# Two chained transformer blocks on one core: affine rows held back, roots as a power on GpSimd, and a new split of transposed rows

## The chip, the core and the metric

The kernel runs on one core of a Trainium2 chip. The metric is the time of the device for one execution, in microseconds (us). The engines are named as in the profile: PE is the matrix engine (TensorE), DVE the vector engine, ACT the scalar engine, POOL is GpSimd, SP issues transfers. Each engine works through its own list of instructions in order; semaphores tie the lists together.

## What is computed

Two blocks are chained over 512 image tokens and 256 context tokens of width 1024, all in float32. Cut to what matters here:

```
# first block, two layers
for i in (0, 1):
    y = mixer_i(modulate(h, m[0], m[1]))             # retention; neighbourhood attention
    h = layer_norm(alpha * h + m[2] * y, ln_g[i, 0], ln_b[i, 0])
    f = swiglu(modulate(h, m[3], m[4]), w13[i], w2[i])   # (silu(a @ gate) * (a @ up)) @ w2
    h = layer_norm(alpha * h + m[5] * f, ln_g[i, 1], ln_b[i, 1])
# second block, one layer
z = rms_norm(x, g_mix) @ w_in                        # windowed and block attention, a linear recurrence
x = x + merged(z) @ w_out
u = rms_norm(x, g_ffn) @ w_gu
x = x + (silu(gate) * up) @ w_down                   # then a last rms_norm

def layer_norm(x, g, b):
    xc = x - mean(x);  return xc * rsqrt(mean(xc * xc) + 1e-5) * g + b
def rms_norm(x, g):
    return x * rsqrt(mean(x * x) + 1e-6) * g
```

The image and the context tokens have their own modulation m; in the second layer of the first block the context's rows are needed only as keys and values.

## The kernel before

**Products.** A float32 product is made of three faster ones. Each operand is split into a high part that the fast format holds exactly and a low part, the rest; `mm3` and `t_mm` add high x high, high x low and low x high in a bank. A weight slab comes as one transfer (`raw`, 128x1024) and is split in two halves: ACT copies the high part, DVE subtracts it (`w<-raw,w`), in some stretches POOL. Eight banks hold results. Tokens stand in six tiles of 128 (0 and 1 context, 2 to 5 image), four where only image tokens are left.

**Order.** `body` does not issue instructions but records them into a `Recorder`. Its `plan` is a list scheduler: an instruction becomes ready when its predecessors have ended by a table of costs (`cost`) and handovers (`LAG`), and each engine takes the earliest in program order among the ready ones; `issue` writes them out in order of the planned starts. So each engine's order is decided by these costs, and all instructions have one line in the profile, that of the replay. `after(n, f)` puts a piece of program n ticks of the clock later (a tick comes after a piece of a product).

**Transitions.** The residual rows are R[i][half], token tile by token tile, and the next products need them normalised and transposed. `bound` runs a row product in two half sweeps. The last slabs of the second run tile by tile, and after each tile a chain of small work follows: `add_gated` (DVE multiplies the bank by the gate, `gt<-bank,gbc`; POOL adds it, `R<-gt,R`), statistics (`bn`, `mv`), `rsqrt`, and the normalised rows (`R<-R,mv,rstd`). `rsqrt` is written for DVE: a first guess from the bits, then three Newton steps, in all eight instructions on 128x1 (`rs_g`, `rs_h`, `rs_t`, `rstd`) behind one that adds eps. In pairs the tiles go to `to_T`: PE transposes (`bank<-ident,R`), ACT scales and shifts (`tt`), DVE casts the high part (`act<-tt`), POOL subtracts the low part (`act<-tt,act`). `t_gemm_first` then multiplies the first slabs by the context part, then by the image part in two halves of 256 columns, so that it can begin before the last pair is there; `r_sweep(first=...)` does the same token tile by token tile.

R itself is kept with the affine of the layer norm, which the next residual needs: `affine_rows` multiplies and adds on POOL (`R<-R,bc`), 128x512 four times a tile. `affine_later` puts it behind the transition by `after`, from the third tick.

The transitions are named here T1 (retention's output product to feed-forward, at 700 us), T2 (feed-forward to neighbourhood attention, 1262), T3 (attention's output to feed-forward, 1640), T4 (first block to second, 2015; here two norms follow each other, a layer norm and an RMS norm, whose rows are `X`, `chain_h`), and T5 (second block's mixer to its feed-forward, 2560).

Of the kernel before, what the change touches and what calls it, by code (L numbers as in the profile page):

```python
# [51 lines left out]
class Recorder:  # L52
# [34 lines left out]
    def add(self, eng, meth, fn, a, k):  # L87
# [5 lines left out]
        for w, aps in ((False, ins), (True, outs)):  # L93
            for ap in aps:
# [18 lines left out]
                keep.append((i, w, r))  # L113
                self.hist[n] = keep
        self.ops.append((eng, meth, fn, a, k, preds, list(dict.fromkeys(names)), i + self.bias))

    LAG = {("vector", "tensor"): 260, ("scalar", "tensor"): 281, ("gpsimd", "tensor"): 203,
# [4 lines left out]
    def cost(self, op):  # L122
# [13 lines left out]
        if eng == "tensor":  # L136
            if meth == "transpose":
                return n / 1.2, 0
            return (max(n * 4 / 2.4, 213) if a[2].dtype == F32 else n / 2.4) + 2.5, 0
        ptr = sum(isinstance(v, bass.AP) for v in k.values())  # L140
# [8 lines left out]
        fast = meth in ("tensor_scalar", "tensor_copy", "memset") and not ps  # L149
        return n / (1.92 if fast else 0.96) + 69 + 60 * ptr, 0  # L150

    def plan(self):
# [40 lines left out]
        win, busy, warm, carry_end = 0, 0.0, False, 0.0  # L193
        start, stop, tfin = [0.0] * N, [0.0] * N, {}

        def push(t, kind, x):
# [15 lines left out]
        while nd < N:  # L212
# [12 lines left out]
            while progressed:  # L225
                progressed = False
                for e in engs:
# [41 lines left out]
                    start[i] = now  # L269
                    end = now + hold  # L270
                    free[e] = end
                    if op[1] == "dma_start":
# [176 lines left out]
def body(nc, tc, io, sp, wp, pp, dp, order, stop=None, dbg=None):  # L449
# [66 lines left out]

    def rsqrt(out, v):
        g = small([128, 1], "rs_g", dt=I32)
        h = small([128, 1], "rs_h")
        t = small([128, 1], "rs_t")  # L520
        DVE.tensor_scalar(g, v.bitcast(I32), -0.5, float(0x5F3759DF), op0=ALU.mult, op1=ALU.add)
        DVE.tensor_scalar(h, v, -0.5, None, op0=ALU.mult)
        y = g.bitcast(F32)
        for it in range(3):
            DVE.scalar_tensor_tensor(t, y, y, h, op0=ALU.mult, op1=ALU.mult)
            DVE.scalar_tensor_tensor(out if it == 2 else y, t, 1.5, y, op0=ALU.add, op1=ALU.mult)

# [18 lines left out]
    ones = kp.tile([128, 128], F32, name="ones", tag="ones", bufs=1)  # L546
    DVE.memset(ones, 1.0)
    ones_r = kp.tile([128, 128], F32R, name="ones_r", tag="ones_r", bufs=1)
    ACT.activation(ones_r, ones, AF.Copy)
# [106 lines left out]
    def t_gemm_first(keys, act, segs):  # L656

        wts = [ws.get(*k) for k in keys]
        parts = []
        for s in segs:  # L660
            if s[0] not in parts:
                parts.append(s[0])
        banks = [out_banks(parts) for _ in keys]
        for part, c0, c1, pre in segs:
            if pre is not None:
                pre()
            for b, w in zip(banks, wts):
# [48 lines left out]

    def add_gated(R, i, half, b, gate):
        if gate is None:
            DVE.tensor_tensor(R[i][half], b, R[i][half], op=ALU.add)
        else:  # L720
            t = S(name="gt")
            DVE.tensor_tensor(t, b, gate[half], op=ALU.mult)
            POOL.tensor_tensor(R[i][half], t, R[i][half], op=ALU.add)

# [7 lines left out]
    def ln_rstd(i):  # L732
        mv = small([128, 2], "mv", bufs=8)
        DVE.bn_aggr(mv, stats[i])
        v = small([128, 1], "lnv", bufs=8)
        DVE.tensor_scalar(v, mv[:, 1:2], 1e-5, None, op0=ALU.add)
        rstd = small([128, 1], "rstd", bufs=8)
        rsqrt(rstd, v)
        return mv, rstd
# [6 lines left out]
    def rms_rows(R, i, n=1024):  # L746
        ss = small([128, 2], "ss", bufs=8)
        for half in range(2):
            j = S(name="sq")
            ACT.activation(j, R[i][half], AF.Square, accum_out=ss[:, half:half + 1])  # L750
        v = small([128, 1], "rv", bufs=8)
        DVE.tensor_tensor(v, ss[:, 0:1], ss[:, 1:2], op=ALU.add)
        DVE.tensor_scalar(v, v, 1.0 / n, 1e-6, op0=ALU.mult, op1=ALU.add)
        rstd = small([128, 1], "rstd", bufs=8)
        rsqrt(rstd, v)
        return rstd
# [8 lines left out]
    def to_T(rows, part, c0, act, G, Bc, grid=False):  # L765

        for kb in range(4):
# [14 lines left out]
            if part == "c":  # L782
                for hl in range(2):
                    act.ctx[kb, hl] = S(F32R, "act")
                DVE.tensor_copy(act.ctx[kb, 0], t)
                POOL.tensor_tensor(act.ctx[kb, 1], t, act.ctx[kb, 0], op=ALU.subtract)
            else:
                for kk in range(2):
# [208 lines left out]
    def ret_av(A, V, g, h, sink):  # L997
        for i, (part, t0) in enumerate(TL0):
# [5 lines left out]
            ss = small([128, 1], "rss", bufs=4)  # L1004
            ACT.activation(sq, b, AF.Square, accum_out=ss)
            DVE.tensor_scalar(ss, ss, 1.0 / 512, 1e-6, op0=ALU.mult, op1=ALU.add)
            rstd = small([128, 1], "rstd", bufs=8)
            rsqrt(rstd, ss)
            yg = S(name="yg")
# [75 lines left out]
    def bound(sweep0, sweep1, R, tiles, gates, chain, segs_T, early=True):  # L1085
# [13 lines left out]
        def on_tile(i):  # L1099
            add_gated(R, i, 1, banks1[i], gates[i])  # L1100
            if early:
# [49 lines left out]
    def ffn1(name, act, parts, j0, j1, first=None):  # L1151
        fT = Acts()
        for j in range(j0, j1):
            if j == 0 and first is not None:
# [22 lines left out]
    affine_later(R, range(6), ga, ba)  # L1177
    for c in (0, 1):
# [7 lines left out]
    for ci, (j0, j1) in enumerate(chunks):  # L1186
# [26 lines left out]

    affine_later(R, range(2, 6), ga, ba, h0_store)
    vd = dp.tile([6, 128, 1024], F32, name="vd", tag="vd")
# [232 lines left out]
    dump("xn2", R[0][0])  # L1448
    affine_later(R, range(4), ga, ba)
    gates = [gate_bc[1, 5, 0]] * 4  # L1450
# [570 lines left out]
```

## Time and profile before

| | |
|---|---|
| median of 3 runs | 2943.53 us (2943.51 to 2943.56) |
| profiled execution, time | 2940.55 us |
| profiled execution, span from first to last instruction | 2938.8 us |
| PE busy | 2849.6 us (97%) |
| DVE, ACT, POOL busy | 1667.2, 1109.8, 702.8 us |
| mean granted clock of PE | 0.990 |

The profiled execution lies 1.75 us around its span and 3.0 us below the median. Busy times overlap; idle time of an engine counts only where another waits for it. The granted clock is the share of full speed (2.4 GHz) that PE was allowed in a stretch; 0.5 is 1.2 GHz.

### The profile page before, as it was taken

To read this page: it belongs to the slowest core of one execution; us is meant where nothing else is said; L and a number is where in the kernel's file an instruction comes from. 1 tells how busy PE (TensorE), PEld (TensorE's weight loads), DVE (VectorE), ACT (ScalarE), POOL (GpSimd) and SP (SyncE) were. 2 spreads that over 40 slices of the span, in tenths; PEclk is the share of its full clock that TensorE was granted. 3 is DMA by queue.
4 is the path that set the end of the run, shared out by engine and by line. 5 is a ranking of instruction groups with operands and counts; after the bars stand their busy time and mean duration, and the time that the engine had idled before them with its cause. 6 is when DMAs were issued, how large, how long until landed. Compare 5 with 4: busy or idle time off the path is not lost. (4 is left out here: it accounts for less than half of the span.)

```text
span 2938.8 us, 37765 instructions
## 1 busy us (share of the span) xinstructions
PE 2849.6 (97%) x13988; PEld 2385.0 (81%) x13988; DVE 1667.2 (57%) x3387; ACT 1109.8 (38%) x2343; POOL 702.8 (24%) x592
## 2 busy tenths in 40 slices
PE   8999999998999999989999899998999999999998
PEld 5788888887988888878787788886888888888887
DVE  8887534536955435384999832337476763642233
ACT  4332333521222222324778322323466743332231
POOL 4312212214412112172220711104333110211100
PEclk9999999999999999999999999999999999999999
DMA  8343202322234324323224222334422223332231
GB/s 321 108 141 107 97 29 87 129 81 99 94 114 141 124 74 154 100 100 110 76 73 128 84 92 78 101 108 148 164 87 90 86 90 107 99 103 79 72 115 43
DMA packets 120463, 311.01 MB, mean 106 GB/s; under 512 B 12646, under 2 KB 22230, under 8 KB 120278
## 3 DMA queue, kind: packets, MB, share of 16 engines
q1 hardware_dynamic: 120278, 308.60, 32.1%
q8 instruction: 110, 1.80, 0.2%
q14 instruction: 75, 0.61, 0.1%
HBM read 292.77 MB, written 22.33 MB: 107 GB/s over the span
## 5 line engine op out<-in xcount | busy, mean ns | idle before, releaser
L321 PE MATMUL bank<-act,w 128*128 128x512 f32 (+1 forms) x6960 | 1427.3, 363 | 9.7 <-ACT act L321 7.4
L321 PEld LDWEIGHTS bank<-act,w 128*128 128x128 f32 x6960 | 1176.3, 189 | 210.6 <-ACT act L321 8.0
L321 DVE TENSOR_TENSOR w<-raw,w 128x512 fp32r<-128x512 f32 x664 | 521.4, 809 | 557.4 <-PE bank L321 346.5
L321 ACT ACTIVATE w<-raw 128x512 fp32r<-128x512 f32 x748 | 439.5, 627 | 512.3 <-PE bank L321 351.6
L321 PE MATMUL bank<-w,act 128*128 128x512 f32 (+1 forms) x1728 | 392.7, 387 | 6.6 <-ACT w L321 4.0
L321 PEld LDWEIGHTS bank<-w,act 128*128 128x128 f32 x1728 | 320.0, 190 | 73.0 <-ACT w L321 4.5
L321 PE MATMUL bank<-w,f 128*128 128x512 f32 x1584 | 364.5, 390 | 0.0
L321 PEld LDWEIGHTS bank<-w,f 128*128 128x128 f32 x1584 | 297.2, 188 | 61.4
L321 POOL TENSOR_TENSOR f<-sg,f 128x512 fp32r<-128x512 f32 x66 | 87.9, 1331 | 511.4 <-ACT f L321 492.1
L321 POOL TENSOR_TENSOR R<-gt,R 128x512 f32<-128x512 f32 x64 | 87.8, 1394 | 379.1 <-DVE gt L321 370.6
L321 POOL TENSOR_TENSOR w<-raw,w 128x512 fp32r<-128x512 f32 x84 | 111.8, 1357 | 178.6 <-ACT w L321 158.9
L321 PE MATMUL bank<-w,yT 128*128 128x512 f32 x576 | 133.7, 393 | 0.0
L321 PEld LDWEIGHTS bank<-w,yT 128*128 128x128 f32 x576 | 108.8, 190 | 22.6
L321 ACT ACTIVATE f<-sg 128x512 fp32r<-128x512 f32 x66 | 41.7, 632 | 225.1 <-DVE sg L321 220.8
L321 DVE TENSOR_TENSOR sg<-bank,sg 128x512 f32<-128x512 f32 x66 | 45.5, 690 | 135.8 <-PE bank L321 135.8
L321 POOL TENSOR_TENSOR act<-tt,act 128x256 fp32r<-128x256 f32 (+1 forms) x88 | 77.4, 908 | 80.0 <-DVE act L321 72.8
L321 ACT ACTIVATE sg<-bank 128x512 f32<-128x512 f32 x66 | 39.5, 598 | 150.6 <-PE bank L321 138.9
L321 ACT ACTIVATE s<-s,nm 128x384 f32<-128x384 f32 (+3 forms) x144 | 79.5, 557 | 28.1 <-DVE nm L321 28.0
L321 ACT ACTIVATE pt<-bank 128x512 fp32r<-128x512 f32 (+3 forms) x176 | 72.5, 469 | 46.6 <-PE bank L321 46.0
L321 DVE TENSOR_TENSOR gt<-bank,gbc 128x512 f32<-128x512 f32 x64 | 43.2, 687 | 81.2 <-PE bank L321 74.9
L321 POOL TENSOR_TENSOR R<-R,bc 128x512 f32<-128x512 f32 x56 | 83.0, 1496 | 13.6 <-PE bank L321 12.1
L321 DVE TENSOR_TENSOR pt<-bank,pt 128x512 fp32r<-128x512 f32 (+3 forms) x176 | 82.0, 519 | 5.9 <-ACT pt L321 5.2
(217 smaller groups left out, 3085.8 us busy)
## 6 DMA issues: line engine op xcount, KB each, us to landing
raw<-w_w SPq DMA_DIRECT2D x132, 512.0 KB, 3.5
aw<-w_ada_t SPq DMA_DIRECT2D x112, 256.0 KB, 4.1
raw<-w_b_gu SPq DMA_DIRECT2D x44, 512.0 KB, 3.5
aw<-w_ada SPq DMA_DIRECT2D x64, 256.0 KB, 4.8
raw<-w_b_gt SPq DMA_DIRECT2D x24, 512.0 KB, 3.5
raw<-w_b_dn SPq DMA_DIRECT2D x22, 512.0 KB, 3.5
raw<-w_ret_qk SPq DMA_DIRECT2D x16, 512.0 KB, 3.6
raw<-w_ret_v SPq DMA_DIRECT2D x16, 512.0 KB, 4.8
```

Source lines behind the costliest of these rows:

```text
L321: ins = fn(*a, **k).ins
```

## The change

Seven things are edited.

1. Instructions recorded between `hold(True)` and `hold(False)` get the newest product as a predecessor. `affine_later` uses this, and its first tick is 13, 7 or 11 in place of 3.
2. `plan` has new costs for the products, and treats POOL's instructions and those of DVE that read two wide operands from SBUF, or copy or scale there, as if they excluded each other (`locks`).
3. `rsqrt` is two POOL instructions, add eps (`rs_e`) and a power of -0.5 (`mhalf`); the mean of the RMS norms is taken into ACT's square.
4. `t_gemm_first` of the three feed-forward layers starts with four slabs instead of two; two slabs' context parts share a bank.
5. The last two tiles of a `bound` add their gated rows on DVE instead of POOL.
6. `to_T` has the high part copied by ACT instead of DVE, and the low part subtracted by DVE instead of POOL (88 each).
7. The first half sweep of `na_v` starts with four slabs instead of two, split ahead of it.

```diff
+        if self.held is not None:
+            preds.add(self.held)
+        if eng == "tensor":
+            self.newest_mm = i
...
-            return (max(n * 4 / 2.4, 213) if a[2].dtype == F32 else n / 2.4) + 2.5, 0
+            if a[2].dtype == F32:
+                return max(n * 4 / 2.4, 213) + 2.5, 0
+            return n * 0.4427 + (0 if n > 400 else 6), 0
...
+    def locks(self, op):
...
+        if eng == "gpsimd":
+            return True
+        if eng != "vector" or meth in ("reciprocal", "bn_stats"):
+            return False
+        if any(v.space == PSUM for v in aps):
+            return False
+        return len(wide) > 2 or meth in ("tensor_scalar", "tensor_copy")
...
+                    if locks[i]:
+                        end = port = max(now, port) + hold
...
-    def rsqrt(out, v):
-        g = small([128, 1], "rs_g", dt=I32)
-        h = small([128, 1], "rs_h")
-        t = small([128, 1], "rs_t")
-        DVE.tensor_scalar(g, v.bitcast(I32), -0.5, float(0x5F3759DF), op0=ALU.mult, op1=ALU.add)
-        DVE.tensor_scalar(h, v, -0.5, None, op0=ALU.mult)
-        y = g.bitcast(F32)
-        for it in range(3):
-            DVE.scalar_tensor_tensor(t, y, y, h, op0=ALU.mult, op1=ALU.mult)
-            DVE.scalar_tensor_tensor(out if it == 2 else y, t, 1.5, y, op0=ALU.add, op1=ALU.mult)
+    def rsqrt(out, v, eps):
+        e = small([128, 1], "rs_e", bufs=8)
+        POOL.tensor_scalar(e, v, eps, None, op0=ALU.add)
+        POOL.tensor_tensor(out, e, mhalf, op=ALU.pow)
...
-        banks = [out_banks(parts) for _ in keys]
+        banks = [out_banks([p for p in parts if p == "l"]) for _ in keys]
+        if "c" in parts:
+            for i in range(0, len(keys), 2):
+                b = bank()
+                for j in range(2):
+                    banks[i + j]["c"] = b[:, j * 256:j * 256 + 256]
...
-            POOL.tensor_tensor(R[i][half], t, R[i][half], op=ALU.add)
+            (eng or POOL).tensor_tensor(R[i][half], t, R[i][half], op=ALU.add)
...
-                    DVE.tensor_copy(hi, src)
-                    POOL.tensor_tensor(lo, src, hi, op=ALU.subtract)
+                    ACT.activation(hi, src, AF.Copy)
+                    DVE.tensor_tensor(lo, src, hi, op=ALU.subtract)
...
-            add_gated(R, i, 1, banks1[i], gates[i])
+            add_gated(R, i, 1, banks1[i], gates[i], DVE if i >= n - 2 else None)
...
-                b = t_gemm_first([(name, 0), (name, NF)], act, first)
-                ffn1_evac(b[0], b[1], fT, j, j0)
-                ws.done(2)
+                    b = t_gemm_first([(name, x) for i in range(2) for x in (i, NF + i)], act, first)
+                    for i in range(2):
+                        ffn1_evac(b[2 * i], b[2 * i + 1], fT, i, j0)
+                    ws.done(4)
...
-    def affine_later(R, idx, ga, ba, then=None):
+    def affine_later(R, idx, ga, ba, then=None, first=3):
         for n, i in enumerate(idx):
             def f(i=i):
+                nc.hold(True)
                 affine_rows(R, i, ga, ba)
+                nc.hold(False)
                 if then is not None:
                     then(i)
-            after(2 * n + 3, f)
+            after(2 * n + first, f)
...
+            ws.depth = 6
...
-        banks = r_sweep("na_v", half * 4, 4, aT, TL0, first=2 if half == 0 else 0, pre=pre, fill=bg)
+        banks = r_sweep("na_v", half * 4, 4, aT, TL0, first=4 if half == 0 else 0, pre=pre, fill=bg)
+        ws.depth = WB
```

On POOL at T1 these rows stood before, from the last sweeps of retention's output product to the first feed-forward slabs; gt is the gated row of a bank, bc the affine's coefficients, act the transposed rows' low part.

```order
61 L321 TENSOR_TENSOR R<-gt,R 128x512 x8
62 L321 TENSOR_TENSOR R<-R,bc 128x512
63 L321 TENSOR_TENSOR R<-gt,R 128x512
64 L321 TENSOR_TENSOR act<-tt,act 128x512 x4
65 L321 TENSOR_TENSOR R<-gt,R 128x512
66 L321 TENSOR_TENSOR R<-R,bc 128x512 x3
67 L321 TENSOR_TENSOR R<-gt,R 128x512
68 L321 TENSOR_TENSOR R<-R,bc 128x512 x2
69 L321 TENSOR_TENSOR act<-tt,act 128x256 x8
70 L321 TENSOR_TENSOR R<-gt,R 128x512
71 L321 TENSOR_TENSOR R<-R,bc 128x512 x5
72 L321 TENSOR_TENSOR act<-tt,act 128x256 x8
```

In the changed kernel the same stretch of POOL reads so; mv holds mean and variance, of which the root is taken.

```order
109 L351 TENSOR_TENSOR R<-gt,R 128x512 x7
110 L351 TENSOR_SCALAR rs_e<-mv 128x1
111 L351 TENSOR_TENSOR rstd<-rs_e,mhalf 128x1
112 L351 TENSOR_TENSOR R<-gt,R 128x512
113 L351 TENSOR_SCALAR rs_e<-mv 128x1
114 L351 TENSOR_TENSOR rstd<-rs_e,mhalf 128x1
115 L351 TENSOR_TENSOR R<-gt,R 128x512
116 L351 TENSOR_SCALAR rs_e<-mv 128x1
117 L351 TENSOR_TENSOR rstd<-rs_e,mhalf 128x1
118 L351 TENSOR_TENSOR R<-gt,R 128x512
119 L351 TENSOR_SCALAR rs_e<-mv 128x1
120 L351 TENSOR_TENSOR rstd<-rs_e,mhalf 128x1
```

No affine row and no low part is left between the gated adds there; each add is followed by the two instructions of a root, and the affine rows stand further down, behind the first rows of f, the hidden values of the feed-forward.

On PE at T4 these rows stood before, from the last product of the first block (w,f) to the first of the second block (w,act); ident,X are the transposes.

```order
1066 L321 MATMUL bank<-w,f 128x512 x492
1067 L321 MATMUL bank<-ident,X 128x128 x4
1068 L321 MATMUL bank<-w,f 128x512 x34
1069 L321 MATMUL bank<-ident,X 128x128 x12
1070 L321 MATMUL bank<-w,f 128x512 x2
1071 L321 MATMUL bank<-hot,tab 20x320
1072 L321 MATMUL bank<-w,act 128x512 x4
1073 L321 MATMUL bank<-w,act 128x256 x2
1074 L321 MATMUL bank<-w,act 128x512 x44
1075 L321 MATMUL bank<-ident,X 128x128 x4
1076 L321 MATMUL bank<-w,act 128x256 x45
1077 L321 MATMUL bank<-ident,X 128x128 x12
```

In the changed kernel the same stretch of PE is:

```order
1019 L351 MATMUL bank<-w,f 128x512 x492
1020 L351 MATMUL bank<-ident,X 128x128 x16
1021 L351 MATMUL bank<-w,f 128x512 x36
1022 L351 MATMUL bank<-hot,tab 20x320 x2
1023 L351 MATMUL bank<-w,act 128x512 x48
1024 L351 MATMUL bank<-ident,X 128x128 x4
1025 L351 MATMUL bank<-w,act 128x256 x35
1026 L351 MATMUL bank<-ident,X 128x128 x12
```

The first sixteen transposes now stand together behind 492 products, with 36 products behind them in one piece, and 48 and 35 others ahead of the last twelve transposes.

On POOL at T4 the changed kernel has these rows, where w is the low part of a weight slab and rv the RMS norm's sum:

```order
287 L351 TENSOR_SCALAR rs_e<-mv 128x1
288 L351 TENSOR_TENSOR rstd<-rs_e,mhalf 128x1
289 L351 TENSOR_SCALAR rs_e<-rv 128x1
290 L351 TENSOR_TENSOR rstd<-rs_e,mhalf 128x1
291 L351 TENSOR_TENSOR w<-raw,w 128x512 x4
292 L351 TENSOR_SCALAR rs_e<-mv 128x1
293 L351 TENSOR_TENSOR rstd<-rs_e,mhalf 128x1
294 L351 TENSOR_TENSOR w<-raw,w 128x512 x4
295 L351 TENSOR_SCALAR rs_e<-rv 128x1
296 L351 TENSOR_TENSOR rstd<-rs_e,mhalf 128x1
297 L351 TENSOR_TENSOR w<-raw,w 128x512 x70
```

Before, POOL's list held no root there; now eight low parts of weights stand between those of the last tile.

## Rows read from the trace of the kernel before

**Rows 1.** Page, part 1: busy us (share of span) and instructions of each engine.
```profile
PE 2849.6 (97%) x13988; PEld 2385.0 (81%) x13988; DVE 1667.2 (57%) x3387; ACT 1109.8 (38%) x2343; POOL 702.8 (24%) x592
```

**Rows 2.** Windows by stage: length, busy us of each engine (instructions), PEclk, DMA.
```profile
74.00:90.00 16.00, 9.29 (x30) 6.04 (x29) 16.00 (x18) 8.73 (x16) 10.80 (x8) 0.79 0.16 40
700.00:742.00 42.00, 31.95 (x183) 28.89 (x182) 39.63 (x75) 11.32 (x24) 32.26 (x31) 0.84 0.33 113
1262.00:1312.00 50.00, 41.49 (x197) 33.91 (x196) 44.16 (x101) 15.07 (x31) 33.28 (x32) 0.97 0.28 100
1320.00:1590.00 270.00, 259.04 (x1438) 215.98 (x1438) 219.71 (x518) 183.40 (x497) 68.67 (x83) 0.99 0.29 94
1640.00:1667.00 27.00, 16.67 (x93) 13.43 (x92) 25.39 (x48) 8.26 (x17) 20.22 (x19) 0.75 0.32 97
2015.00:2060.00 45.00, 33.52 (x159) 27.77 (x158) 44.02 (x113) 18.52 (x45) 29.96 (x29) 0.85 0.66 240
2560.00:2585.00 25.00, 22.55 (x153) 20.06 (x152) 22.52 (x52) 13.13 (x30) 14.25 (x16) 1.00 0.19 62
2600.00:2900.00 300.00, 300.00 (x1325) 248.51 (x1324) 88.89 (x126) 85.07 (x149) 25.80 (x20) 1.00 0.26 83
```

**Rows 3.** Eight PE windows of low clock: length, busy (instructions), granted clock, DMA share.
```profile
1583.08:1586.49 3.41, 3.41 (x15) 0.50 0.00 0
...
2023.40:2033.64 10.24, 8.15 (x25) 0.50 0.49 177
2054.12:2057.53 3.41, 3.30 (x15) 0.50 0.99 349
sum 54.62, PE 39.88; mean PE 4.98
```

**Rows 4.** Timeline at T1: start, us, engine, operation, output and inputs, count, [idle before].
```profile
702.75 1.00 DVE L321 TENSOR_SCALAR R<-R,mv,rstd 128x512 f32<-128x512 f32 x2
703.67 0.68 DVE L321 TENSOR_TENSOR gt<-bank,gbc 128x512 f32<-128x512 f32 x1
...
704.43 1.27 POOL L321 TENSOR_TENSOR R<-gt,R 128x512 f32<-128x512 f32 x1 [2.63 <-DVE gt L321]
...
706.47 0.21 DVE L321 BATCH_NORM_AGGREGATE mv<-bn 128x2 f32<-128x12 f32 x1
...
714.75 3.76 ACT L321 ACTIVATE tt<-bank,cB,cG 128x256 f32<-128x256 f32 x8 [16.25 <-PE bank L321]
...
721.10 5.92 PE L321 MATMUL bank<-act,w 128*128 128x256 f32 x48
...
726.33 6.93 POOL L321 TENSOR_TENSOR R<-R,bc 128x512 f32<-128x512 f32 x5
...
728.24 1.22 DVE L321 SCALAR_TENSOR_TENSOR rs_t<-rs_g,rs_h 128x1 f32<-128x1 f32 x1
...
734.36 2.82 PE L321 MATMUL bank<-ident,R 128*128 128x128 f32 x12 [3.67 <-DVE R L321]
```

**Rows 5.** Timeline of PE from 74 to 90.
```profile
80.50 1.49 PE L321 MATMUL bank<-w,act 128*128 128x512 f32 x4 [4.03 <-ACT w L321]
84.50 5.76 PE L321 MATMUL bank<-w,act 128*128 128x512 f32 x16 [2.52 <-DVE w L321]
```

**Rows 6.** Single tiles' instructions by engine: count, ns minimum/median/maximum, first and last start.
```profile
L321 POOL TENSOR_TENSOR act<-tt,act x88: 727/788/1489, 696.2 to 2581.7; 128x256 fp32r<-128x256 f32 x80, 128x512 fp32r<-128x512 f32 x8
...
L321 DVE SCALAR_TENSOR_TENSOR rs_t<-rs_g,rs_h x168: 198/220/1316, 162.8 to 2933.9; 128x1 f32<-128x1 f32 x168
...
L321 DVE TENSOR_TENSOR w<-raw,w x664: 625/691/1831, 46.9 to 2882.3; 128x512 fp32r<-128x512 f32 x166
```

**Rows 7.** Timeline at T4.
```profile
2013.91 9.39 POOL L321 TENSOR_TENSOR w<-raw,w 128x512 fp32r<-128x512 f32 x6
...
2026.83 1.41 DVE L321 SCALAR_TENSOR_TENSOR R<-R,rstd,bc 128x512 f32<-128x512 f32 x2
...
2028.54 0.64 ACT L321 ACTIVATE sq<-R 128x512 f32<-128x512 f32 x1
```

More of the change, by code (lines that the diff above doesn't have):

```diff
@@ L70, in __init__ @@
         self.bias = 0
+        self.held, self.newest_mm = None, None
         for n in ("tensor", "vector", "scalar", "gpsimd", "sync"):
@@ L114, in add, with hold @@
                 self.hist[n] = keep
+        if self.held is not None:
+            preds.add(self.held)
+        if eng == "tensor":
+            self.newest_mm = i
         self.ops.append((eng, meth, fn, a, k, preds, list(dict.fromkeys(names)), i + self.bias))
+    def hold(self, on):
+        self.held = self.newest_mm if on else None
     LAG = {("vector", "tensor"): 260, ("scalar", "tensor"): 281, ("gpsimd", "tensor"): 203,
@@ L150, in cost @@
         return n / (1.92 if fast else 0.96) + 69 + 60 * ptr, 0
+    def locks(self, op):
+        eng, meth, _, a, k = op[:5]
+        aps = [v for v in a if isinstance(v, bass.AP)] + [v for v in k.values() if isinstance(v, bass.AP)]
+        wide = [v for v in aps if v.ap[-1][1] > 4 and v.space != PSUM]
+        if meth == "dma_start" or not wide:
+            return False
[4 more added lines that the diff above has]
+        if any(v.space == PSUM for v in aps):
+            return False
+        return len(wide) > 2 or meth in ("tensor_scalar", "tensor_copy")
     def plan(self):
@@ L194, in plan @@
         start, stop, tfin = [0.0] * N, [0.0] * N, {}
+        locks = [self.locks(op) for op in ops]
+        port = 0.0
         def push(t, kind, x):
@@ L547, in body @@
     DVE.memset(ones, 1.0)
+    mhalf = kp.tile([128, 1], F32, name="mhalf", tag="mhalf", bufs=1)
+    DVE.memset(mhalf, -0.5)
     ones_r = kp.tile([128, 128], F32R, name="ones_r", tag="ones_r", bufs=1)
@@ L714, in r_sweep, with add_gated @@
         return banks
-    def add_gated(R, i, half, b, gate):
+    def add_gated(R, i, half, b, gate, eng=None):
         if gate is None:
@@ L734, in ln_rstd @@
         DVE.bn_aggr(mv, stats[i])
-        v = small([128, 1], "lnv", bufs=8)
-        DVE.tensor_scalar(v, mv[:, 1:2], 1e-5, None, op0=ALU.add)
         rstd = small([128, 1], "rstd", bufs=8)
-        rsqrt(rstd, v)
+        rsqrt(rstd, mv[:, 1:2], 1e-5)
         return mv, rstd
@@ L749, in rms_rows @@
             j = S(name="sq")
-            ACT.activation(j, R[i][half], AF.Square, accum_out=ss[:, half:half + 1])
+            ACT.activation(j, R[i][half], AF.Square, scale=n ** -0.5, accum_out=ss[:, half:half + 1])
         v = small([128, 1], "rv", bufs=8)
         DVE.tensor_tensor(v, ss[:, 0:1], ss[:, 1:2], op=ALU.add)
-        DVE.tensor_scalar(v, v, 1.0 / n, 1e-6, op0=ALU.mult, op1=ALU.add)
         rstd = small([128, 1], "rstd", bufs=8)
-        rsqrt(rstd, v)
+        rsqrt(rstd, v, 1e-6)
         return rstd
@@ L784, in to_T @@
                     act.ctx[kb, hl] = S(F32R, "act")
-                DVE.tensor_copy(act.ctx[kb, 0], t)
-                POOL.tensor_tensor(act.ctx[kb, 1], t, act.ctx[kb, 0], op=ALU.subtract)
+                ACT.activation(act.ctx[kb, 0], t, AF.Copy)
+                DVE.tensor_tensor(act.ctx[kb, 1], t, act.ctx[kb, 0], op=ALU.subtract)
             else:
@@ L1004, in ret_av @@
             ss = small([128, 1], "rss", bufs=4)
-            ACT.activation(sq, b, AF.Square, accum_out=ss)
-            DVE.tensor_scalar(ss, ss, 1.0 / 512, 1e-6, op0=ALU.mult, op1=ALU.add)
+            ACT.activation(sq, b, AF.Square, scale=512 ** -0.5, accum_out=ss)
             rstd = small([128, 1], "rstd", bufs=8)
-            rsqrt(rstd, ss)
+            rsqrt(rstd, ss, 1e-6)
             yg = S(name="yg")
@@ L1153, in ffn1 @@
         for j in range(j0, j1):
-            if j == 0 and first is not None:
-                b = t_gemm_first([(name, 0), (name, NF)], act, first)
-                ffn1_evac(b[0], b[1], fT, j, j0)
-                ws.done(2)
+            if j < 2 and first is not None:
+                if j == 0:
+                    b = t_gemm_first([(name, x) for i in range(2) for x in (i, NF + i)], act, first)
+                    for i in range(2):
+                        ffn1_evac(b[2 * i], b[2 * i + 1], fT, i, j0)
+                    ws.done(4)
                 continue
@@ L1167, in ffn1 @@
         return fT
-    def affine_later(R, idx, ga, ba, then=None):
+    def affine_later(R, idx, ga, ba, then=None, first=3):
         for n, i in enumerate(idx):
             def f(i=i):
+                nc.hold(True)
                 affine_rows(R, i, ga, ba)
+                nc.hold(False)
                 if then is not None:
                     then(i)
-            after(2 * n + 3, f)
-    affine_later(R, range(6), ga, ba)
+            after(2 * n + first, f)
+    affine_later(R, range(6), ga, ba, first=13)
     for c in (0, 1):
@@ L1212, in h0_store @@
             nc.sync.dma_start(h0d[(i - 2) * 128:(i - 1) * 128, half * 512:half * 512 + 512], R[i][half])
-    affine_later(R, range(2, 6), ga, ba, h0_store)
+    affine_later(R, range(2, 6), ga, ba, h0_store, first=7)
     vd = dp.tile([6, 128, 1024], F32, name="vd", tag="vd")
@@ L1448, in body @@
     dump("xn2", R[0][0])
-    affine_later(R, range(4), ga, ba)
+    affine_later(R, range(4), ga, ba, first=11)
     gates = [gate_bc[1, 5, 0]] * 4
```

## The prediction

> **What bounds the kernel now.** The page's totals come first [rows 1]: PE is busy for 2849.6 of 2938.8 us, so PE bounds the kernel, and only 89.2 us of idle time can be won by order alone. The windows by stage say where these lie [rows 2]: subtract PE's busy time from each window's length. From 2600 to 2900 nothing is left (300.00 of 300 us, 1325 matmuls, 226 ns each). The first products on values leave 6.7 us (74 to 90). The transitions, where rows are normalised, transposed and fed to the next products, leave 10.1 us (T1, 700 to 742), 8.5 (T2, 1262), 10.3 (T3, 1640), 11.5 (T4, 2015) and 2.5 (T5, 2560). Neighbourhood attention (1320 to 1590) leaves 11.0.
>
> Then the granted clock. In eight windows it is 0.50 [rows 3], that is 1.2 instead of 2.4 GHz; the windows by stage show that they fall where PE had waited (clock 0.79, 0.84, 0.75, 0.85). PE is busy in them for 39.88 us, of which half, 19.9 us, would not be spent at full clock. Idle and clock together: 109 us.
>
> What PE waits for at T1 is seen in the timeline [rows 4]. It waits 3.67 us for DVE's R. Before that DVE works through the small 128x1 steps of a root; one takes 1.22 us where the shortest of its kind takes 0.198 [rows 6], and at that moment POOL runs five affine rows, 6.93 us. Beside POOL the ordinary low-part split on DVE stretches likewise, 0.625 to 1.831 us [rows 6]. The Trainium skill ("SBUF — State Buffer", Who interferes with whom) says that POOL shares a port pair with DVE, and that a DVE instruction with two SBUF inputs is held while POOL reads; the trace agrees with it on the 1.22 us step.
>
> **The change, part by part.** The sum is made against the profiled execution, 2940.55 us; the median is 2943.53, so 3.0 us are added at the end.
>
> Start (ordering by the plan's new costs): the weight copies for the value products move ahead of the decay strips on ACT and DVE. PE's two waits there, 4.03 us for ACT's w and 2.52 us for DVE's [rows 5], go; I leave 0.5: gain 6.1.
>
> T1. The affine rows (56 in all, five of them 6.93 us here) leave the transition; POOL there keeps R<-gt and two 128x1 operations a root. The chain of one token tile becomes: from gt's start to the end of the aggregate 3.01 us (703.67 to 706.47 + 0.21, with POOL's add between) [rows 4], two POOL operations, then two norm steps 1.00 us [rows 4]. No 128x1 operation on POOL stands in the trace. The nearest row is its 128x256 subtraction, at least 0.727 us [rows 6]; below, 0.198 us, the shortest step of that size on DVE. Between these I take 0.35 each, nearer to the size than to the engine, since a 128x512 POOL row takes 1.27 [rows 4] against 0.727 for half of it: most of the time goes with the columns. With 0.3 us for handovers the chain is 3.01 + 0.7 + 1.0 + 0.3 = 5.0 us. Its cover is the next tile's 24 products, 24 x 0.226 = 5.4 us. So PE need hardly wait; the last tile has 96 products of 256 columns over it (5.92 us for 48 [rows 4], 11.8). I leave 1.5 us: gain 8.6. T3 has the same tiles: gain 10.3 - 1.5 = 8.8.
>
> What covers the new ACT copies: scaled and high part of a 128x256 piece now both come from ACT. The scaled one takes 0.47 us (3.76 us for eight [rows 4]); I take the copy, of the same shape, as long: 0.94. With four slabs PE has 12 products of 0.123 us a piece, 1.48 us. With two slabs it would be 0.74, less than ACT needs. That is what the larger first group buys; it costs 48 products of 512 columns turned into 96 of 256: 48 x (2 x 0.123 - 0.226) = 1.0 us, in three places, 3.0 at most; I take 1.8, as the 256-column time includes the start of its group.
>
> T2. A tile has 18 products, 4.1 us, but DVE takes the next tile's gt before this tile's norm, so that its loop is some 3 us: 2 us stay, gain 6.5.
>
> T4. A tile's chain has a second half: two scaled adds 1.41 us beside the roots and two more behind them, a square of 0.64 with its handovers (1.1 in all; the other runs beside the add) [rows 7], a second root and two X rows, near the 1.00 us of the two norm steps: 3.01 + 1.4 + 1.4 + 1.1 + 0.7 + 1.0 = 8.6 us against 36 products, 8.1. And the order shows what is not repaired: eight low parts on POOL stand between the last tile's roots. Six of them took 9.39 us [rows 7]; eight would be 12.5 where none has run yet, of which I count half. Before the last transposes stand 48 products of 512 and 35 of 256 columns, 10.8 + 4.3 = 15.1 us, and the chain has 8.6 + 6.3 + some 3 for DVE's splits in between = 18. I leave 1.5 + 3 + 1.4 (for a second handover) = 5.9: gain 5.6.
>
> T5 and the readout of the last retention heads: roots only. Eight small steps, three of them of 0.22 us (median [rows 6]), with the handovers some 2 us, become two of 0.35: 1 us each, 2.0 in all.
>
> Neighbourhood attention: the new costs reorder it, with no operation taken away; DVE is busy 219.71 of 270 us [rows 2]. Zero, with 8 us to either side.
>
> The affine rows themselves, 56 x 1.27 = 71 us on POOL [rows 4], are hidden behind the feed-forward products, where DVE has 88.89 us of work in 300 (the window from 2600 stands for these, [rows 2]); without that cover they would come back as waits for f, two or three microseconds at each of three places.
>
> Clock: the gaps that precede the low windows shrink to a microsecond or two. I keep two low windows, those behind 1583 (attention, not touched) and 2054 (T4): 3.41 and 3.30 us of busy time [rows 3], half of it 3.4 us. Gain 19.9 - 3.4 = 16.5.
>
> Sum: 6.1 + 8.6 + 8.8 + 6.5 + 5.6 + 2.0 + 16.5 - 1.8 = 52.3 us. 2940.55 - 52.3 = 2888.3, as a median 2891.
>
> One rule is weighed against this. The Trainium skill (same page and section) would have the low parts, which go from POOL to DVE as two-input subtractions, stand in line with any POOL reader; by it T4, where 70 POOL splits follow, would lose again. From rows alone: DVE's split of 512 columns has 0.625 and 1.831 us as its ends [rows 6], so a piece may lose up to 1.2 us, and sixteen pieces at T4 19 us on DVE, part of it under the 15 us of products. This is in the first rival.
>
> **The rivals.** *Half the gain stays away.* The chains are serial on DVE, gt to X before the next gt, and where before 46 or more products lay between two transposes of a pair, at T4 the cover is now 36. If the POOL operations take 0.73 us each, T1 and T3 chains are 5.8 us against 5.4 (0.4 for each of eight tiles, 3 us), T4's is 9.4 (1.3 for each of three, 4 us), and the splits at T4 contend: its 11.5 us stay. That takes 3 + 5.6 off, and the low clock at T4 stays (8.15 us busy from 2023 [rows 3], half 4): 52 - 3 - 6 - 4 - 6 for a worse order in attention = 33, 2910 as a median. For it: DVE is busy 44.02 of 45 us at T4 [rows 2]. Against: much of that was steps beside POOL's affine and split rows.
>
> *Slower: the power.* If eps and power together take P on POOL, a serial chain grows by P - 0.7, at T4 by twice that. T1 has five exposed intervals, T2 five, T3 three, T4 three with two roots, T5 three: 22 roots. With slack of 0.4 us a tile at T1 and T3 and 1 us at T2, 9 us in all, the gain of 52 us is eaten at 0.7 + 61/22 = 3.5 us, and at 2.8 if the low clock stays as well (16 us less to eat). At P = 5 it is 22 x 4.3 - 9 = 86 us, 2977. For it: DVE's own root was written in eight steps rather than one, and no power is in the trace. Against: the longest of POOL's 88 low parts, of 256 or 512 columns, takes 1.489 us [rows 6], and a root has one element a partition.
>
> *Nothing changes.* The affine rows and low parts were covered after all, and the gaps come from chain latency that stays: then T1's wait of 3.67 us behind a stretched root would not end the very moment that R is ready [rows 4]. The time would be 2940 to 2947.
>
> *More than forecast.* T4 and attention come out clean as well: 5.9 + 3.4 + 8 us more, 2874.
>
> **How the numbers follow.** The likeliest is the sum, with chance 0.5 (2880 to 2902); half the gain 0.25 (2902 to 2925); more than forecast 0.14; no change 0.05; slower by the power 0.06. The range of 8 in 10 runs from 2872 to 2918, cutting the upper part of the half-gain case and both cases of no gain. A measurement of this kernel tells 0.2%, 6 us, from no change. Faster 0.90, the same 0.04, slower 0.06.
>
> **What would show it.** Right: at T1 no POOL affine row between the last products of ret_out and the first of the feed-forward, and PE idle there under 3 us, clock above 0.95; the same at T3; no wait for w near 80 us. POOL's rs_e and rstd rows each under 0.75 us show the root; T4's idle of 6 us ends on DVE's X. Wrong: an rstd row of several microseconds, DVE's act<-tt pieces at 1.2 us and more, PE idle in attention beyond 14 us, or low clock windows at T1, T2 or T3.

## The result, and the profile after

The changed kernel takes 2893.3 us (median of 4 runs, 2891.88 to 2895.42) against 2943.52 before: ratio 0.9834, 95% interval 0.982 to 0.9847. The forecast was 2891. The sum came out, but by errors that nearly cancel: T2 and attention gave less than forecast, T4 more, and the reason given for T1 and T3 was only half right.

The page of the changed kernel, engines' busy time, beside [rows 1]:

```profile
PE 2837.0 (98%) x14132; PEld 2380.7 (82%) x14132; DVE 1539.5 (53%) x2892; ACT 1136.9 (39%) x2431; POOL 677.8 (23%) x608
```

The span is 2890.1 us, so PE idles for 53.1 instead of 89.2 us, and is busy 12.6 us less: 48.7 us in all. The windows by stage (length, busy time of PE, PEld, DVE, ACT and POOL, granted clock, DMA) answer to [rows 2]; the stages lie earlier now:

```profile
74.00:90.00 16.00, 16.00 (x73) 13.23 (x72) 16.00 (x22) 7.21 (x11) 8.00 (x5) 1.00 0.18 61
676.00:722.00 46.00, 46.00 (x298) 41.82 (x297) 29.02 (x62) 22.72 (x54) 9.11 (x14) 1.00 0.35 126
1245.00:1295.00 50.00, 41.80 (x182) 32.43 (x181) 34.97 (x48) 23.77 (x53) 28.76 (x27) 0.90 0.25 78
1300.00:1570.00 270.00, 255.11 (x1427) 213.58 (x1426) 216.49 (x524) 183.02 (x499) 62.36 (x78) 0.99 0.30 98
1615.00:1645.00 30.00, 29.89 (x225) 28.41 (x224) 21.11 (x44) 20.42 (x46) 2.25 (x4) 1.00 0.39 107
1960.00:2010.00 50.00, 48.22 (x244) 39.29 (x243) 38.87 (x75) 24.02 (x61) 24.32 (x26) 1.00 0.36 130
2510.00:2540.00 30.00, 29.94 (x216) 27.87 (x215) 16.50 (x38) 17.22 (x46) 3.08 (x6) 1.00 0.16 54
```

T1, T3 and T5 have no idle time left that counts, T4 has 1.8 us, and the value slabs at 74 to 90 no longer wait. T2 keeps 8.2 of its 8.5 us, and attention has 14.9 where it had 11.0.

The root on POOL, of the list of one tile's instructions (count, ns minimum, median, maximum):

```profile
L351 POOL TENSOR_TENSOR rstd<-rs_e,mhalf x56: 555/567/1057, 155.0 to 2885.1; 128x1 f32<-128x1 f32 x56
...
L351 POOL TENSOR_SCALAR rs_e<-mv x20: 213/222/778, 675.3 to 1998.5; 128x1 f32<-128x1 f32 x20
```

Add and power take 0.222 + 0.567 = 0.79 us; the prediction took 0.7 for the pair. At T1 the chain of one token tile, from gt to the normalised rows, now reads:

```profile
677.57 0.69 DVE L351 TENSOR_TENSOR gt<-bank,gbc 128x512 f32<-128x512 f32 x1 [0.41 <-PE bank L351]
...
681.60 1.00 DVE L351 TENSOR_SCALAR R<-R,mv,rstd 128x512 f32<-128x512 f32 x2 [1.00 <-POOL rstd L351]
```

At T2 the waits of before are nearly gone. They were four, together all of its 8.5 us, each for DVE's normalised R; the longest was this row of the kernel before:

```profile
1289.55 2.82 PE L321 MATMUL bank<-ident,R 128*128 128x128 f32 x12 [3.31 <-DVE R L321]
```

One wait of that kind, 0.80 us, is left. What took their place is seen in the changed kernel's timeline (start, duration, engine, operation, count, idle time before and what ended it):

```profile
1265.66 22.65 POOL L351 TENSOR_TENSOR R<-R,bc 128x512 f32<-128x512 f32 x16
1265.73 2.93 DVE L351 TENSOR_SCALAR R<-R,mv,rstd 128x512 f32<-128x512 f32 x2 [1.00 <-POOL rstd L351]
1268.58 5.14 DVE L351 TENSOR_TENSOR w<-raw,w 128x512 fp32r<-128x512 f32 x3
1269.55 1.91 PE L351 MATMUL bank<-ident,R 128*128 128x128 f32 x16
...
1273.64 2.90 DVE L351 TENSOR_TENSOR act<-tt,act 128x256 fp32r<-128x256 f32 x2
1275.18 0.96 PE L351 MATMUL bank<-w,act 128*128 128x512 f32 x3 [2.79 <-DVE act L351]
...
1284.36 1.02 ACT L351 ACTIVATE tt<-bank,cB,cG 128x256 f32<-128x256 f32 x2 [6.09 <-POOL R L351]
...
1285.73 1.22 PE L351 MATMUL bank<-w,act 128*128 128x512 f32 x2 [3.86 <-ACT act L351]
```

All sixteen affine rows, which were to stand behind the products, start in the moment in which the last tile is normalised. Beside them the two norm steps take 2.93 us (1.00 alone, [rows 4]), three splits 5.14 and two low parts of the transposed rows 2.90. ACT's scaled part, which takes 1.02 us for two as elsewhere, waits 6.09 us until POOL is through most of its rows. So PE waits twice for different reasons, 2.79 us for DVE's stretched steps and 3.86 for ACT, which POOL holds up, and two of the five low clock windows of this kernel follow (below). The Trainium skill ("SBUF — State Buffer", Who interferes with whom) has tensor_scalar among what can contend with POOL, and says that ACT waits on nobody's port; the trace agrees: beside POOL's rows DVE's pair went from 1.00 to 2.93 us, while ACT's pair stayed at 1.02. ACT's 6.09 us are a wait for POOL's work to be done, not a stretched instruction.

PE's windows of low clock in the changed kernel, beside [rows 3]:

```profile
10.52:20.76 10.24, 5.29 (x20) 0.50 1.04 395
109.50:112.92 3.42, 3.42 (x9) 0.50 0.00 0
1276.86:1280.28 3.42, 3.42 (x9) 0.50 0.01 2
1283.69:1290.52 6.83, 4.50 (x9) 0.50 0.01 2
1560.17:1567.00 6.83, 5.06 (x21) 0.50 0.00 0
sum 30.74, PE 21.70; mean PE 4.34
```

39.88 us of busy time at 1.2 GHz have become 21.70. None is left at T1, T3 and T4.

### The profile page after: what moved, and what is told of

Its sections match the earlier page's. It is cut to its first block, busy times and chain, and to the rows that moved or that the text cites. A ratio compares the mean times of both kernels' runs of the same rounds, so it can differ in the third digit from the quotient of the medians.

```text
span 2890.1 us, 37677 instructions
## 1 busy us (share of the span) xinstructions
PE 2837.0 (98%) x14132; PEld 2380.7 (82%) x14132; DVE 1539.5 (53%) x2892; ACT 1136.9 (39%) x2431; POOL 677.8 (23%) x608
## 5 line engine op out<-in xcount | busy, mean ns | idle before, releaser
L351 DVE TENSOR_TENSOR w<-raw,w 128x512 fp32r<-128x512 f32 x664 | 504.3, 782 | 573.6 <-PE bank L351 354.6
L351 POOL TENSOR_TENSOR R<-gt,R 128x512 f32<-128x512 f32 x56 | 78.6, 1423 | 358.5 <-DVE gt L351 357.9
L351 ACT ACTIVATE pt<-bank 128x384 fp32r<-128x384 f32 (+3 forms) x176 | 71.8, 470 | 53.3 <-PE bank L351 52.5
L351 DVE TENSOR_TENSOR pt<-bank,pt 128x384 fp32r<-128x384 f32 (+3 forms) x176 | 81.7, 517 | 6.3 <-ACT pt L351 5.5
L351 PE MATMUL bank<-v,A 128*128 128x512 f32 x336 | 81.4, 395 | 0.0
```

The source lines that it names most:

```text
L351: ins = fn(*a, **k).ins
```

## The experiments

Each run is set beside the kernel before on its own chip by a ratio. The table has PE's idle time by stretch, in us, from each run's trace (length less busy time; "values" is 17 to 140 us, "heads" from there to T1, each T from 8 us ahead of its first transposes to 25 behind its last, "NA" from T2 to T3).

| run | ratio (95%) | values | heads | T1 | T2 | NA | T3 | T4 | T5 |
|---|---|---|---|---|---|---|---|---|---|
| before | 1 | 8.5 | 2.9 | 10.0 | 8.5 | 11.0 | 10.5 | 11.5 | 2.5 |
| changed | 0.9834 (0.982 to 0.9847) | 3.3 | 1.1 | 0.0 | 8.2 | 15.0 | 0.1 | 1.8 | 0.1 |
| hold_waits | 0.9798 (0.9783 to 0.9812) | 3.3 | 1.1 | 0.0 | 0.8 | 14.5 | 0.1 | 2.0 | 0.1 |
| undo_affine | 0.9819 (0.9803 to 0.9835) | 4.5 | 1.1 | 3.3 | 0.8 | 13.4 | 1.6 | 2.0 | 0.1 |
| undo_root | 0.986 (0.9845 to 0.9874) | 3.3 | 1.5 | 0.3 | 6.8 | 12.4 | 0.1 | 9.7 | 0.1 |
| undo_affine_root | 0.989 (0.9875 to 0.9905) | 3.3 | 1.5 | 7.3 | 1.6 | 13.4 | 4.5 | 9.8 | 0.1 |
| undo_split | 0.9823 (0.9808 to 0.9838) | 4.5 | 1.1 | 0.0 | 1.1 | 20.1 | 0.0 | 3.9 | 0.0 |
| undo_first | 0.9839 (0.9823 to 0.9856) | 3.3 | 1.1 | 0.9 | 8.8 | 15.3 | 0.9 | 2.0 | 0.0 |
| undo_plan | 0.9853 (0.9838 to 0.9868) | 9.8 | 0.7 | 0.0 | 8.6 | 12.4 | 0.1 | 4.7 | 0.1 |
| root_only | 0.9953 (0.9938 to 0.9968) | 9.5 | 0.6 | 7.2 | 6.8 | 11.3 | 5.3 | 11.5 | 1.1 |
| root_plan | 0.9895 (0.988 to 0.9909) | 3.3 | 1.1 | 3.6 | 3.0 | 16.0 | 7.0 | 9.0 | 0.0 |
| hold_no_port | 0.9864 (0.9849 to 0.9878) | 7.6 | 1.1 | 0.0 | 2.3 | 16.5 | 0.1 | 6.8 | 0.1 |
| hold_old_cost | 0.9788 (0.9773 to 0.9802) | 5.4 | 0.5 | 0.0 | 0.3 | 17.2 | 0.1 | 1.1 | 0.1 |
| power_six | 1.0123 (1.0106 to 1.014) | 3.3 | 26.2 | 8.7 | 9.4 | 13.1 | 5.0 | 21.5 | 5.2 |

Every edit is planned anew, so an edit also reorders stretches that it does not touch; attention moves between 11 and 20 us that way. Parts 5 and 7 of the change (the last adds on DVE, the larger first group of `na_v`) were not undone by themselves, and the held rows were not tried alone on the kernel before.

**hold_waits: the hold as a real wait.** In the changed kernel `hold` adds a predecessor for `plan` only; `issue` ties instructions to the order of their engine and tiles. So the affine rows have a place, not a wait.

```diff
+            self.real[i] = self.held
...
+            named[i] = ins.name
...
+            if i in self.real:
+                tc.add_manual_dep(ins, named[self.real[i]], SYNC, reason="held")
```

> The changed kernel, but the held affine rows get a real wait for the held product; nothing else differs in the plan. Theory (the hold is only a place in the order, and at T2 nothing on POOL stands ahead of the affine rows, so they start beside the last norm): PE's idle time at T2 falls from 8.2 us to under 3 us, the two low clock windows at 1277 and 1284 go, and the time falls by 8 to 11 us, to about 2884. Rival (ACT, which now copies scaled and high parts, paces the first attention products): T2 keeps its 7 us and the time stays within 2 us of 2893.

2881.56 us, some 10 us below the changed kernel by the ratios. The same stretch of its timeline:

```profile
1266.50 1.00 DVE L353 TENSOR_SCALAR R<-R,mv,rstd 128x512 f32<-128x512 f32 x2 [1.00 <-POOL rstd L353]
1270.32 1.91 PE L353 MATMUL bank<-ident,R 128*128 128x128 f32 x16
...
1271.99 28.19 PE L353 MATMUL bank<-w,act 128*128 128x512 f32 x121
...
1297.38 4.35 POOL L353 TENSOR_TENSOR R<-R,bc 128x512 f32<-128x512 f32 x3 [30.91 <-PE bank L353]
```

POOL now stands 30.91 us and starts when PE releases it; the norm steps take 1.00 us, three splits 1.89 and two low parts 0.76, and PE runs 121 products without a break. T2's idle time falls from 8.2 to 0.8 us, and no low clock window is left there. The theory holds, and the rival falls, since ACT's copies are the same in both. The run takes DVE's stretched steps and ACT's wait away together, so it does not say what each costs. That ACT's 6.09 us were a wait for a buffer that the thirteenth affine row gives back fits the time of its end, but is only argued.

**undo_affine: affine rows as before.**

```diff
-                nc.hold(True)
                 affine_rows(R, i, ga, ba)
-                nc.hold(False)
...
-    affine_later(R, range(6), ga, ba, first=13)
+    affine_later(R, range(6), ga, ba)
```

The two other calls lose their `first` likewise, so that the first tick is 3 again.

> The changed kernel with the affine rows as before: not held, from the third tick. Theory (the affine rows on POOL stretched the chain beside them): idle time comes back at T1, T2 and T3, 10 us or more in all, with low clock windows behind it, so 12 to 25 us slower than the changed kernel. Rival (the roots' move and the plan's costs did it): under 5 us slower, T1 and T3 still without a wait.

2886.86 us, ratio 0.9819: not slower than the changed kernel, T1 with 3.3 us, T3 with 1.6, T2 clean. The theory fell: in the changed kernel the held rows are not needed to keep T1 and T3 nearly open. POOL does run affine rows in T1, eight from 703.80, 11.29 us in all, of which this window shows six, and DVE's steps beside them stretch as at T2:

```profile
703.80 8.45 POOL L351 TENSOR_TENSOR R<-R,bc 128x512 f32<-128x512 f32 x6
703.87 2.94 DVE L351 TENSOR_SCALAR R<-R,mv,rstd 128x512 f32<-128x512 f32 x2 [0.43 <-POOL rstd L351]
...
706.73 4.37 DVE L351 TENSOR_TENSOR act<-tt,act 128x256 fp32r<-128x256 f32 x3
```

But PE has 35 products over the norm, and its 3.3 us are seven waits of at most 0.67. At T2 the last norm takes 1.00 us: the last eight affine rows must wait for its transposes there, and start at 1279.54, behind it.

**undo_root: eight steps on DVE again**, the body of `rsqrt` as in the diff's minus lines, behind an add of eps on DVE.

> The changed kernel with the root as eight steps on DVE again, all else as changed. Theory (with the affine rows gone, a root costs 2 us on DVE against 0.8 us on POOL): chains get 1.2 to 1.5 us a root longer, of which the slack at T1 and T3 hides most: 3 to 9 us slower, most of it at T2, T4 and T5. Rival (the power is what opened T1 and T3): over 12 us slower, waits for R at T1 and T3.

2899.68 us, 0.986. The loss stands at T4, where one wait for X is 6.67 us; T1 and T3 stay clean. The theory's size held, about 8 us, though not its share for T2, and its rival fell.

**undo_affine_root: both of these edits.**

> The changed kernel with the affine rows as before and the root as eight steps on DVE again; plan's costs, split, first groups stay changed. Theory (either cure alone relieves T1 and T3, since what hurt was DVE's small steps beside POOL's affine rows): idle time at T1 and T3 comes back, 8 us or more, and T2 and T4 as with the root undone: over 15 us slower than the changed kernel, 2905 or more. Rival (T1 and T3 were opened by the plan's costs, the split or the first groups): T1 and T3 stay under 3 us, the time near that of the root undone alone, 2894 to 2902.

2910.04 us, 0.989: 7.3 us come back at T1 and 4.5 at T3. Its timeline at T1 shows what [rows 4] showed before:

```profile
694.11 1.22 DVE L351 SCALAR_TENSOR_TENSOR rs_g<-rs_t,rs_g 128x1 f32<-128x1 f32 x1
...
695.27 3.84 POOL L351 TENSOR_TENSOR R<-R,bc 128x512 f32<-128x512 f32 x3
...
697.82 1.30 DVE L351 SCALAR_TENSOR_TENSOR rs_t<-rs_g,rs_h 128x1 f32<-128x1 f32 x1
...
699.96 0.60 PE L351 MATMUL bank<-ident,R 128*128 128x128 f32 x2 [3.51 <-DVE R L351]
```

So within the changed kernel either cure is nearly enough at T1 and T3, and waits of several microseconds need both ills: small steps on DVE and wide rows on POOL beside them. The theory holds. On the kernel before it is not so; see root_only.

**undo_split: transposed rows split as before**, `tensor_copy` on DVE for the high and POOL for the low part.

> The changed kernel with the transposed rows split as before (high part cast by DVE, low part by POOL). Theory: low parts of 0.73 us on POOL queue ahead of the next roots, 2 to 6 us slower, waits for act at T2 to T5. Rival (DVE and POOL have both room once the affine rows are away): within 2 us of the changed kernel.

2889.14 us, 0.9823, within the interval of the changed kernel. At T2 the idle time falls to 1.1 us, but an 8.0 us wait for ACT's vs stands in attention instead:

```profile
1286.28 17.40 POOL L351 TENSOR_TENSOR R<-R,bc 128x512 f32<-128x512 f32 x12
...
1300.64 0.63 ACT L351 ACTIVATE w<-raw 128x512 fp32r<-128x512 f32 x1 [17.06 <-POOL R L351]
...
1304.88 5.30 PE L351 MATMUL bank<-w,act 128*128 128x512 f32 x12 [7.98 <-ACT vs L351]
```

ACT waits 17.06 us for POOL's last twelve affine rows, and its vs come behind that: it is T2's loss, moved a little further down. The theory fell and the rival holds by the time: the new split is worth nothing that these runs can show by itself, though T4 has 3.9 against 1.8 us.

**undo_first: two slabs in the first group.**

```diff
-                    b = t_gemm_first([(name, x) for i in range(2) for x in (i, NF + i)], act, first)
+                    b = t_gemm_first([(name, 0), (name, NF)], act, first)
```

> The changed kernel with two slabs instead of four in the first group of the three feed-forward layers. Theory (ACT's two copies of a piece, 0.94 us by estimate, pace two slabs, 0.74 us a piece): waits for act of 1 to 2 us at each of T1, T3 and T5, 2 to 6 us slower. Rival (ACT is fast enough, and fewer products are cut in halves): 0 to 2 us faster.

2895.1 us, 0.9839, the same as the changed kernel. T1 and T3 show 0.9 us each, less than the theory's 1 to 2, and the wait is another than it said:

```profile
703.74 5.92 PE L351 MATMUL bank<-act,w 128*128 128x256 f32 x48
709.49 0.27 PE L351 MATMUL bank<-ident,R 128*128 128x128 f32 x1
710.64 1.86 PE L351 MATMUL bank<-ident,R 128*128 128x128 f32 x15 [0.88 <-DVE R L351]
```

The 48 products run without a wait for ACT's copies; PE waits for DVE's R behind them, since the last tile has half the products over it. The theory fell, and the rival, a gain, does not show either.

**undo_plan: old product costs, no port rule.**

```diff
-            return n * 0.4427 + (0 if n > 400 else 6), 0
+            return n / 2.4 + 2.5, 0
...
-        locks = [self.locks(op) for op in ops]
+        locks = [False for op in ops]
```

> The changed kernel planned with the old costs of products and without the port rule. Theory: the two waits for the first value slabs (6.5 us and a low clock window behind them) come back, attention goes back to 10 us of idle, T1 and T3 stay without waits: 3 to 8 us slower. Rival (the plan opened T1 and T3): over 15 us slower, waits at T1 and T3.

2899.19 us, 0.9853. The waits for the first value slabs are back (9.8 against 3.3 us), T1 and T3 stay clean: 5.6 us slower by the ratios, as the theory had it, though attention went back to 12.4 us only, not 10.

**root_only and root_plan: parts of the change on the kernel before**, first the root alone, then with the plan's costs and port rule.

> The kernel before with one part of the change alone: roots as two operations on POOL. Theory (with the affine rows still ahead in POOL's list, a root waits behind them, 1.3 us each): T1, T2, T3 keep half of their idle time, T4 and the readouts gain: 10 to 20 us faster than before. Rival (the root's small steps on DVE were the whole of the loss): 30 us faster or more, T1 and T3 under 2 us of idle time.

2928.76 us, 0.9953, 14 us: T1 keeps 7.2 us and T3 5.3, with no small step of a root left on DVE. What stretches there is the norm itself, beside affine rows:

```profile
707.24 2.67 POOL L321 TENSOR_TENSOR R<-R,bc 128x512 f32<-128x512 f32 x2
707.30 2.89 DVE L321 TENSOR_SCALAR R<-R,mv,rstd 128x512 f32<-128x512 f32 x2 [1.13 <-POOL rstd L321]
...
708.84 3.33 PE L321 MATMUL bank<-ident,R 128*128 128x128 f32 x15 [3.31 <-DVE R L321]
```

The theory holds for T1 and T3 by their times; how much of the rest is roots that queue behind affine rows and low parts on POOL was not taken apart. T4 did not gain, 11.5 us as before; there the expectation was wrong.

> The kernel before with two parts of the change: roots on POOL, and the plan's new costs and port rule. Theory (the start and T1, T3 need these two only; T4 needs the low parts off POOL and the adds on DVE as well): T1 and T3 under 3.5 us, no waits near 80 us, T4 still 6 us or more: 25 to 35 us faster than before. Rival (held rows or the new split are needed for T1 and T3): T1 and T3 keep 5 to 7 us, 15 to 22 us faster.

2911.47 us, 0.9895, 31 us faster than before. T1 falls to 3.6 us, T3 stays at 7.0, T4 at 9.0 (a wait of 6.45 us for X). The time, the values, T1 to within 0.1 us and T4 go with the theory; T3 goes with the rival. T4 needs more parts than root and plan; which of the others was not tried alone.

**hold_no_port and hold_old_cost: the two parts of the plan apart**, each on hold_waits, with one of the two edits of undo_plan.

> The kernel with the real wait, planned without the port rule but with the new costs of products. Theory (the new product costs, not the port rule, moved the first value slabs ahead): no wait for w near 80 us, the idle time in attention 11 to 13 us instead of 14.5: 0 to 3 us faster than with the real wait alone. Rival (the port rule moved them): 5.5 us of waits come back at 78 to 87 us, 5 to 9 us slower.

2902.18 us, 0.9864 against 0.9798: some 19 us slower. PE's timeline has the wait of [rows 5] again:

```profile
79.04 1.54 PE L353 MATMUL bank<-w,act 128*128 128x512 f32 x6
84.57 5.88 PE L353 MATMUL bank<-w,act 128*128 128x512 f32 x12 [3.99 <-DVE w L353]
```

T4 has 6.8 instead of 2.0 us as well. The theory fell, the rival holds: the port rule moved the slabs. Its size does not: 19 us against 5 to 9, since T4 loses too and PE's busy time grows by 5.8 us.

> The kernel with the real wait, planned with the old costs of products but with the port rule. Theory: the waits for the first value slabs come back (5 to 6 us and a low clock window), 6 to 9 us slower than with the real wait. Rival (the port rule moved the slabs): no such waits, within 2 us.

2880.06 us, 0.9788, the same as hold_waits within the intervals, without a wait from 74 to 90. The theory fell here too: the new costs of products bring nothing that shows.

**power_six: the price of the power**, the power taken six times in a row, on hold_waits.

```diff
-        POOL.tensor_tensor(out, e, mhalf, op=ALU.pow)
+        for _ in range(6):
+            POOL.tensor_tensor(out, e, mhalf, op=ALU.pow)
```

> The kernel with the real wait, and the power taken six times in a row for each root (the result is the same), so that add and powers take 3.6 us on POOL instead of 0.8. The prediction's count (22 serial chains, each longer by 2.8 us, less 9 us of slack): 53 us slower than with the real wait, near 2935. Rival (the next tile's product and the last tile's longer cover hide more than counted): 15 to 30 us slower, with most of the waits at T4.

2978.33 us, ratio 1.0123: slower than before, and (1.0123 - 0.9798) x 2942 = 96 us slower than hold_waits. Both expectations were too low. Against hold_waits, T1 to T5 gain 49.8 - 3.0 = 46.8 us of idle time, near the 53 that the count of 22 chains gave. What the count left out is as large: the readouts of the retention heads (26.2 against 1.1 us), the tail, whose idle time grew by 4.2 us, and 21.3 us of PE's busy time (2855.5 against 2834.2).

## Why the prediction came out, point by point

- **The sum**: forecast 52.3 us for the profiled execution, measured 48.7 us of span. It was right by terms that err to both sides: T2, attention, the clock and the start fell short by some 13 us, T1, T3, T4, T5 and the readouts went over by some 9. That they nearly cancel is luck. Some of the prediction's own signs of being wrong came up: attention idles beyond 14 us (14.9), low clock windows stand at T2, and there two of DVE's act<-tt pieces take 2.90 us.
- **Start**: forecast 6.1; the two waits of [rows 5] are gone as it said, 6.7 us in 74 to 90, and a new one of 1.85 us for DVE's v at 106.67 with a low clock window behind it takes a part back. The cause was the plan's port rule, not its costs of products.
- **T1 and T3**: forecast 8.6 and 8.8, measured 10.1 and 10.2. The reading of the 1.22 us step was right, and the chain of 5.0 us against 5.4 us of cover was, too (677.57 to 682.60 above). The attribution was half right: in the new order neither the affine rows' leaving (3.3 and 1.6 us idle without it) nor the root's move (0.3 and 0.1) is needed, only one of them (7.3 and 4.5 without both). The plan has a share at T1 that the prediction did not count: 7.2 us with the root alone, 3.6 with root and plan. And the larger first group does not buy time for ACT's copies, as the prediction had it, but cover for the last tile (undo_first waits 0.88 and 0.76 us for R).
- **T2**: forecast 6.5, measured 0.3. This step failed, though the chain did shrink as forecast: the waits for R fell from 8.5 to 0.80 us, where 2 were forecast to stay. New ones, 7.4 us, came beside the affine rows. The prediction took "the affine rows leave the transition" from POOL's order at T1, where rows of f stand ahead of them, and carried it to T2, where only the last root does. It priced a place in the order as a wait. hold_waits gives 8.2 - 0.8 = 7.4 us back, close to the forecast term.
- **T4**: forecast 5.6, measured 9.7. The first wait for X, 1.62 us, is the 1.5 that was left there; the 4.4 us for the last tile behind eight weight splits did not come. The splits took 12.5 us, as forecast, but the roots behind them waited only 1.0 us for POOL, not 6.3 (half of the splits): the first of the two stood ready at 1997.53 and started at 1998.53, the second came after the last split had ended. The chain from gt (1992.96) to X (2007.64) took 14.7 us, not 18, and PE's products over it, 12.0 and 4.4 us, lasted until it was through, though the second pair of scaled adds took 3.48 us instead of 1.41. The root is needed for it (9.7 us idle without), and is not enough (11.5 with the root alone). Rows of the last tile:

```profile
1995.57 2.99 POOL L351 TENSOR_TENSOR w<-raw,w 128x512 fp32r<-128x512 f32 x2 [3.08 <-ACT w L351]
...
1997.33 0.20 DVE L351 BATCH_NORM_AGGREGATE mv<-bn 128x2 f32<-128x12 f32 x1
...
1998.53 0.21 POOL L351 TENSOR_SCALAR rs_e<-mv 128x1 f32<-128x1 f32 x1
...
1999.66 6.07 POOL L351 TENSOR_TENSOR w<-raw,w 128x512 fp32r<-128x512 f32 x4
1999.84 3.48 DVE L351 SCALAR_TENSOR_TENSOR R<-R,rstd,bc 128x512 f32<-128x512 f32 x2
...
2005.84 0.22 POOL L351 TENSOR_SCALAR rs_e<-rv 128x1 f32<-128x1 f32 x1
```

- **T5 and readouts**: forecast 2.0, measured 2.4 + 1.8 = 4.2. "Roots only" does not hold: with the root back on DVE, undo_root still has 0.1 us at T5 and 1.5 in the heads, where it was 2.5 and 2.9 before.
- **Attention**: forecast 0 within 8 to either side, measured 3.9 us lost. No single undoing brings it back to 11.0 (undo_plan and undo_root 12.4); which part of the new order costs it stays open.
- **Clock**: forecast 16.5 less 1.8 for split products, 14.7; PE's busy time fell by 12.6. The low windows alone give (39.88 - 21.70) / 2 = 9.1, since they stand at three places where the forecast had none (10.5, 109.5 and T2); the other 3.5 us of busy time I did not trace to rows. A low window at the start stands in five of the ten profiles with the new costs of products and in none of the four with the old ones; whether order or chance makes it stays open.
- **Rivals**: "half the gain stays away" and "nothing changes" fell on T1, T3 and T4. "Slower by the power" had the right mechanism and too high a threshold: on a line between hold_waits (0.79 us, 59 us faster than before) and power_six (0.222 + 6 x 0.548 = 3.51 us, 36 us slower) the gain is eaten near 2.5 us, not 3.5, an estimate, since the heads' readouts were not counted.

## What to carry to other kernels

A small chain between two products is priced by what runs beside it, not by its own instructions alone: look for the wide instruction of a neighbour whose span covers the stretched ones, and try moving either away: in the changed kernel one of the two was nearly enough, on the old order the root alone was not. A planner's predecessor holds only while something ahead in the same engine's list waits; where nothing does, make it a real wait, here worth 10 us. And undo parts in pairs before naming the one that helped: here neither of two single undoings showed what both together did.

## What was not expected of the hardware

One power of a 128x1 column on POOL takes 0.567 us and an add of a constant 0.222, where a 128x256 subtraction takes at least 0.727 [rows 6]: the power costs more than twice the add at one element a partition. In T4 the same add took 0.78 us while DVE worked on R<-R,mv,bc (at 1964.6, two rows of 1.41 us together), its longest in the list above, so the stretching seems to go both ways; no run took that apart.
